# Storing the last column group in two large DMAs, and loading the last weight tile whole, in a windowed matrix product

## The chip, the cores and the metric

The kernel runs on one core of a Trainium2 chip. The metric is the time of one execution on the device, in microseconds (us). The profile of an execution gives a "span", from the first to the last instruction, which is 1.6 to 1.7 us shorter than that time. Engines are called TensorE (matrix products; PE in the profile), VectorE (DVE), ScalarE (ACT), GpSimd (POOL) and SyncE (SP); a "q" behind a name means the engine's instruction stream, where DMAs are issued and semaphores are waited for. A core has 16 DMA engines.

## The reference

```python
x: (4, 4096, 4096) float32;  w: (4096, 4096) float32;  offsets: 4 integers
for b in range(4):
    o = int(offsets[b])
    result[b] = x[b, o:o+64] @ w          # 64 rows of each batch, times the whole of w
```

There are 4 x 64 = 256 rows to multiply. All of `w` (67 MB) has to be read once, so this is work for the DMA engines.

## The kernel before

Two batches share a tile of 128 rows, so there are two row groups `g`. `w` is read as float32 and cast to float16 by the DMA itself, in tiles of 128 rows (`k`) by 2048 columns. There are two column groups `ng` of 2048 columns; each accumulates over 32 `k` tiles in all eight PSUM banks. Loads go through GpSimd's queue. The ends of the two column groups are handled differently: the first is copied to `stage` and stored from GpSimd's queue, behind the last load; the last `k` tile of the second is loaded as four column slices, and each slice is multiplied, copied and stored on its own.

```python
    wlast = []
    for ng in range(n_ng):                       # 2 column groups
        for ki in range(n_k):                    # 32 k tiles
            if (ng, ki) in wh:
                continue
            if ng == n_ng - 1 and ki == n_k - 1:
                for j in range(n_sub):           # the last tile: four slices of 512 columns
                    cs = ng * NG + j * NT
                    t = wl_pool.tile([P, NT], fp16, name=f"wl{j}")
                    nc.gpsimd.dma_start(out=t[:], in_=w[ki * P : (ki + 1) * P, cs : cs + NT])
                    wlast.append(t)
            else:
                wh[(ng, ki)] = load(ng, ki)      # [128, 2048], on GpSimd's queue
    # ... transposes of x; the products of all tiles but the last; the first group's copies to stage ...
    for g in range(G):
        nc.gpsimd.dma_start(out=out[2 * g : 2 * g + 2, :, 0:NG], in_=stage[g][:])
    ki = n_k - 1
    q = [nc.scalar, nc.sync]
    for j in range(n_sub):
        cs = (n_ng - 1) * NG + j * NT
        for g in range(G):
            mm(g, j, ki, wlast[j][:], False, True)
            s = sth_pool.tile([P, NT], fp32, name="sth", tag="sth")
            if g == 0:
                nc.scalar.copy(out=s[:], in_=ps[4 * g + j][:])
            else:
                nc.vector.tensor_copy(out=s[:], in_=ps[4 * g + j][:])
            q[g].dma_start(out=out[2 * g : 2 * g + 2, :, cs : cs + NT], in_=s[:])
```

## Time and profile before

| | |
|---|---|
| time, median of 3 runs | 184.98 us (184.97 to 185.01) |
| span of the profiled execution, which took 184.73 us | 183.1 us |
| TensorE busy | 69% of the span |
| DMA queue of GpSimd | 97% of the DMA engines' span |
| a weight tile of 512 KB lands every | 2.44 us |
| TensorE's work for it | 1.89 us |

The page of the kernel before: the busy tenths of TensorE and of the DMA engines in 40 equal slices of the span, what the DMA engines moved in each, and the chain of waits that ended last, by engine and by line.

```profile
PE   0004799988877777887779878777777877777600
DMA  6999999999999999999999999999999999999994
GB/s 179 348 221 215 207 213 215 215 214 211 213 211 214 215 213 214 214 216 214 211 214 212 213 213 214 213 215 214 215 213 212 213 214 212 213 213 205 387 403 172
...
DMA 90%; issue 2%; ACT 1%; PE 1%; ACTq 1%; POOLq 0%
DMA wh<-in_w_dram 90%; ACT sth L150 1%; PE bank L117 1%; ACTq L153 1%; POOLq L60 0%; POOLq L168 0%
```

The DMA engines are full from the second slice to the last but one; TensorE is not. 90% of the chain is waiting for weight tiles to land. (The GB/s count float16 bytes of a load, half of what is read; that is why the figure doubles when the stores come.)

The timeline of TensorE at the end of the kernel before (start, duration, what ran, what ended the idle time before):

```profile
166.48 1.89 PE L117 MATMUL bank<-wh,xT 128*128 128x512 f16 x8 [0.52 <-DMA wh<-in_w_dram]
168.93 1.89 PE L117 MATMUL bank<-wh,xT 128*128 128x512 f16 x8 [0.57 <-DMA wh<-in_w_dram]
170.65 1.89 PE L117 MATMUL bank<-wl,xT 128*128 128x512 f16 x8
```

Each tile is multiplied at once when it lands, then TensorE idles for half a microsecond. Each of the four slices (`wl`) had landed before TensorE came to it, the last at 171.50 us.

The timeline of the DMA issues for the last group in the kernel before (start, duration of the issue):

```profile
171.69 0.34 ACTq L153 DMA_DIRECT2D out_dram<-sth  x1
172.69 0.35 ACTq L153 DMA_DIRECT2D out_dram<-sth  x1
173.69 0.37 ACTq L153 DMA_DIRECT2D out_dram<-sth  x1
174.71 0.34 ACTq L153 DMA_DIRECT2D out_dram<-sth  x1
172.01 2.12 SPq L153 DMA_DIRECT2D out_dram<-sth  x4
```

The DMA queues of the kernel before from 170 to 175 us, then from 175 to 180 us (packets, MB, share of 16 engines' time). q0 is GpSimd's, q10 ScalarE's and q1 SyncE's:

```profile
q0 software_dynamic: 358, 2.06, 104.0%
q10 hardware_dynamic: 8, 0.02, 0.8%
```

```profile
q10 hardware_dynamic: 519, 0.96, 49.7%
q1 hardware_dynamic: 506, 0.94, 48.5%
q0 software_dynamic: 24, 0.10, 4.8%
```

Though the small stores were issued from 171.7 us on, nearly none of their packets ran before 175 us: until then q0 had the engines with the first group's 2.1 MB.

The stretches view of the kernel before, two microseconds a row (the last two columns are the share of the DMA engines and GB/s):

```profile
core 0: us, PE busy (x) PEld busy (x) DVE busy (x) ACT busy (x) POOL busy (x), PEclk, DMA share, GB/s
170.00:172.00 2.00, 2.00 (x11) 0.93 (x10) 0.71 (x2) 0.58 (x1) 0.00 (x0) 1.00 1.11 400
172.00:174.00 2.00, 0.54 (x3) 0.05 (x1) 1.77 (x3) 1.17 (x2) 0.00 (x0) 1.00 1.03 434
174.00:176.00 2.00, 0.00 (x0) 0.00 (x0) 0.00 (x0) 0.58 (x1) 0.00 (x0) 0.72 0.96 392
176.00:178.00 2.00, 0.00 (x0) 0.00 (x0) 0.00 (x0) 0.00 (x0) 0.00 (x0) 0.50 1.06 409
178.00:180.00 2.00, 0.00 (x0) 0.00 (x0) 0.00 (x0) 0.00 (x0) 0.00 (x0) 0.50 1.04 400
180.00:182.00 2.00, 0.00 (x0) 0.00 (x0) 0.00 (x0) 0.00 (x0) 0.00 (x0) 0.50 0.25 93
```

The tail is full: about 400 GB/s until 180 us. Last, the waits of SyncE's instruction stream at the end of the kernel before (line waiting, what for; us in total, times, longest). L179 is the end of the program, where SyncE waits for every DMA to have landed:

```profile
SPq L179 <- DMA out_dram<-sth: 4.5, 1, 4.5
SPq L179 <- DMA out_dram<-stage: 2.9, 1, 2.9
SPq L179 <- PEq L179: 0.7, 2, 0.5
```

### The profile page before, as it was taken

What the parts mean: (1) busy time and instruction counts of PE and PEld (TensorE: products, weight loads), DVE (VectorE), ACT (ScalarE), POOL (GpSimd) and SP (SyncE); (2) the same over time, 40 slices, a digit from 0 to 9 for tenths busy, and PEclk for the clock granted to TensorE, in tenths of its full rate; (3) what the DMA queues carried; (4) which work ended last, traced back from release to release, by engine and by line L of the source; (5) the groups of instructions that cost most, each with busy time, mean ns of one, the idle gap of its engine ahead of it and who ended that gap; (6) DMA issues with size and microseconds to landing.
All of it is one profiled execution on the core that took longest, in us unless ns stands there. A gap on an engine that the chain in (4) does not pass through costs nothing.

```text
span 183.1 us, 1380 instructions
## 1 busy us (share of the span) xinstructions
PE 126.3 (69%) x576; PEld 56.4 (31%) x576; DVE 10.5 (6%) x16; ACT 14.1 (8%) x19; POOL 38.3 (21%) x77
## 2 busy tenths in 40 slices
PE   0004799988877777887779878777777877777600
PEld 0004664433333233333324333323232333333200
DVE  0002530000000000000005000000000000000500
ACT  2081430000000000000013000000000000000310
POOL 4612221222222112222221222222122222210000
PEclk9999999999999999999999999999999999999965
DMA  6999999999999999999999999999999999999994
GB/s 179 348 221 215 207 213 215 215 214 211 213 211 214 215 213 214 214 216 214 211 214 212 213 213 214 213 215 214 215 213 212 213 214 212 213 213 205 387 403 172
DMA packets 11271, 40.97 MB, mean 224 GB/s; under 512 B 1282, under 2 KB 1794, under 8 KB 10626
## 3 DMA queue, kind: packets, MB, share of 16 engines
q0 software_dynamic: 9968, 36.70, 97.0%
q10 hardware_dynamic: 720, 3.15, 4.7%
q1 hardware_dynamic: 578, 1.05, 1.5%
q8 instruction: 4, 0.07, 0.1%
q14 instruction: 1, 0.01, 0.0%
HBM read 71.30 MB, written 4.19 MB: 412 GB/s over the span
## 4 chain that ended last, share of the span: by engine, by line
DMA 90%; issue 2%; ACT 1%; PE 1%; ACTq 1%; POOLq 0%
DMA wh<-in_w_dram 90%; ACT sth L150 1%; PE bank L117 1%; ACTq L153 1%; POOLq L60 0%; POOLq L168 0%
## 5 line engine op out<-in xcount | busy, mean ns | idle before, releaser
L117 PE MATMUL bank<-wh,xT 128*128 128x512 f16 x488 | 113.8, 378 | 28.6 <-DMA wh<-in_w_dram 28.6
L117 PEld LDWEIGHTS <-xT 128*128 128x128 f16 x512 | 49.8, 97 | 98.0 <-issue 44.1
L60 POOL DMA_DIRECT2D wh<-in_w_dram x61 | 32.4, 531 | 112.5 <-DMA wh<-in_w_dram 100.2
L103 PE MATMUL bank<-identity,xrow 128*128 128x128 f16 x64 | 7.1, 311 | 17.4 <-DMA xrow<-in_x_dram 17.4
L103 PEld LDWEIGHTS <-xrow 128*128 128x128 f16 x64 | 6.7, 147 | 17.6 <-issue 17.6
L150 ACT COPY sth<-bank 128x512 f32<-128x512 f32 x4 | 2.3, 586 | 74.6 <-PE bank L117 73.8
L137 ACT COPY stage<-bank 128x512 f32<-128x512 f32 x4 | 2.1, 600 | 70.5 <-PE bank L117 70.5
L112 DVE CAST xT<-bank 128x512 f16<-128x512 f32 x8 | 5.5, 691 | 19.3 <-PE bank L103 19.3
L152 DVE COPY sth<-bank 128x512 f32<-128x512 f32 x4 | 2.5, 683 | 72.3 <-PE bank L117 72.3
L139 DVE COPY stage<-bank 128x512 f32<-128x512 f32 x4 | 2.5, 682 | 71.7 <-PE bank L117 71.7
L114 ACT CAST xT<-bank 128x512 f16<-128x512 f32 x8 | 4.7, 586 | 6.9 <-PE bank L103 6.9
L117 PE MATMUL bank<-w0half,xT 128*128 128x512 f16 x16 | 4.3, 390 | 0.2 <-DVE stage L139 0.2
L90 POOL DMA_DIRECT2D wl<-in_w_dram x4 | 2.1, 527 | 7.5 <-DMA wh<-in_w_dram 7.5
L77 POOL DMA_DIRECT2D xrow<-in_x_dram x4 | 2.1, 520 | 2.2 <-issue 2.2
L97 ACT CAST w0half<-w0row 128x2048 f16<-128x2048 f32 x1 | 1.9, 1897 | 7.4 <-DMA w0row<-in_w_dram 7.4
L141 POOL DMA_DIRECT2D out_dram<-stage x2 | 1.1, 534 | 4.2 <-DMA wh<-in_w_dram 4.2
L98 ACT CAST w0half<-w0row 128x2048 f16<-128x2048 f32 x1 | 1.9, 1893 | 0.0
L117 PE MATMUL bank<-wl,xT 128*128 128x512 f16 x8 | 1.9, 379 | 0.0
L97 ACT ACT_TABLE_LOAD x1 | 1.3, 1283 | 1.3 <-PEq L168 1.3
masks.py:199 POOL TENSOR_SCALAR_AFFINE_SELECT identity<-identity 128x128 f16<-128x128 f16 x1 | 0.3, 287 | 0.1
masks.py:197 POOL MEMSET identity<- 128x128 f16 x1 | 0.2, 223 | 0.0
L168 POOL MEMSET const-float32-0.0<- 128x1 f32 x1 | 0.1, 98 | 0.4 <-issue 0.4
(3 smaller groups left out, 0.3 us busy)
## 6 DMA issues: line engine op xcount, KB each, us to landing
wh<-in_w_dram POOLq DMA_DIRECT2D x61, 512.0 KB, 19.1
w0row<-in_w_dram ACTq DMA_DIRECT2D x1, 2048.0 KB, 9.0
xrow<-in_x_dram POOLq DMA_DIRECT2D x4, 512.0 KB, 12.3
out_dram<-stage POOLq DMA_DIRECT2D x2, 1024.0 KB, 12.1
out_dram<-sth ACTq DMA_DIRECT2D x4, 256.0 KB, 6.5
out_dram<-sth SPq DMA_DIRECT2D x4, 256.0 KB, 6.6
wl<-in_w_dram POOLq DMA_DIRECT2D x4, 128.0 KB, 14.9
off_t<-in_offsets_dram SPq DMA_DIRECT2D x1, 0.0 KB
```

The source lines that it names most:

```text
L60: nc.gpsimd.dma_start(out=t[:], in_=w[ki * P : (ki + 1) * P, ng * NG : (ng + 1) * NG])
L77: nc.gpsimd.dma_start(out=x16[g][m * WIN : (m + 1) * WIN, :], in_=x[b][bass.ds(o, WIN), :])
L90: nc.gpsimd.dma_start(out=t[:], in_=w[ki * P : (ki + 1) * P, cs : cs + NT])
L97: nc.scalar.copy(out=w0_16[:, :NG], in_=w0_32[:, :NG])
L103: nc.tensor.matmul(out=ps[t][:, i * P : (i + 1) * P], lhsT=x16[g][:, k * P : (k + 1) * P], rhs=identity[:], start=True, stop=True,)
L112: nc.vector.tensor_copy(out=dst, in_=ps[t][:])
L114: nc.scalar.copy(out=dst, in_=ps[t][:])
L117: nc.tensor.matmul(out=ps[4 * g + j][:], lhsT=xT[g][:, ki * P : (ki + 1) * P], rhs=rhs, start=start, stop=stop,)
L137: nc.scalar.copy(out=dst, in_=ps[4 * g + j][:])
L139: nc.vector.tensor_copy(out=dst, in_=ps[4 * g + j][:])
L150: nc.scalar.copy(out=s[:], in_=ps[4 * g + j][:])
L152: nc.vector.tensor_copy(out=s[:], in_=ps[4 * g + j][:])
```

## The change

The intent is fewer and larger DMAs at the end: the last `k` tile comes as one 512 KB load with 4 KB rows in SBUF, and the last column group is copied to a staging tile and stored as two 1 MB DMAs with 8 KB rows. The price is that its stores are issued later. The first group's stores stay where they are, on GpSimd's queue behind the last load.

```diff
-            if ng == n_ng - 1 and ki == n_k - 1:
-                for j in range(n_sub):
-                    ... four loads of 512 columns ...
-            else:
+            if (ng, ki) not in wh:
                 wh[(ng, ki)] = load(ng, ki)
 ...
-    stage = [st_pool.tile([P, NG], fp32, name=f"stage{g}") for g in range(G)]
+    stage = [[st_pool.tile([P, NG], fp32, name=f"stage{ng}{g}") for g in range(G)] for ng in range(n_ng)]
+    q = [nc.scalar, nc.sync]
     for ng in range(n_ng):
         last = ng == n_ng - 1
-        for ki in range(n_k - 1 if last else n_k):
+        for ki in range(n_k):
             ... products ...
-        if not last:
-            ... eight copies to stage ...
-    for g in range(G):
-        nc.gpsimd.dma_start(out=out[2 * g : 2 * g + 2, :, 0:NG], in_=stage[g][:])
-    ... for each slice and g: product, copy to sth, store of 512 columns on q[g] ...
+        ... eight copies to stage[ng] ...
+        for g in range(G):
+            (q[g] if last else nc.gpsimd).dma_start(
+                out=out[2 * g : 2 * g + 2, :, ng * NG : (ng + 1) * NG],
+                in_=stage[ng][g][:],
+            )
```

More of the change, by code (lines that the diff above doesn't have):

```diff
@@ L38 @@
     wh_pool = ctx.enter_context(tc.tile_pool(name="wh", bufs=24))
-    wl_pool = ctx.enter_context(tc.tile_pool(name="wl", bufs=1))
     st_pool = ctx.enter_context(tc.tile_pool(name="st", bufs=1))
-    sth_pool = ctx.enter_context(tc.tile_pool(name="sth", bufs=8))
     psum_pool = ctx.enter_context(tc.tile_pool(name="ps", bufs=1, space=bass.MemoryType.PSUM))
@@ L80 @@
         )
-    wlast = []
     for ng in range(n_ng):
         for ki in range(n_k):
-            if (ng, ki) in wh:
-                continue
-            if ng == n_ng - 1 and ki == n_k - 1:
-                for j in range(n_sub):
-                    cs = ng * NG + j * NT
-                    t = wl_pool.tile([P, NT], fp16, name=f"wl{j}")
-                    nc.gpsimd.dma_start(
-                        out=t[:], in_=w[ki * P : (ki + 1) * P, cs : cs + NT]
-                    )
-                    wlast.append(t)
-            else:
+            if (ng, ki) not in wh:
                 wh[(ng, ki)] = load(ng, ki)
@@ L123, in mm @@
         )
-    stage = [st_pool.tile([P, NG], fp32, name=f"stage{g}") for g in range(G)]
+    stage = [
+        [st_pool.tile([P, NG], fp32, name=f"stage{ng}{g}") for g in range(G)]
+        for ng in range(n_ng)
+    ]
+    q = [nc.scalar, nc.sync]
     for ng in range(n_ng):
         last = ng == n_ng - 1
-        for ki in range(n_k - 1 if last else n_k):
+        for ki in range(n_k):
             for g in range(G):
@@ L131 @@
                     mm(g, j, ki, wh[(ng, ki)][:, j * NT : (j + 1) * NT], ki == 0, ki == n_k - 1)
-        if not last:
-            for j in range(n_sub):
-                for g in range(G):
-                    dst = stage[g][:, j * NT : (j + 1) * NT]
-                    if g == 0:
-                        nc.scalar.copy(out=dst, in_=ps[4 * g + j][:])
-                    else:
-                        nc.vector.tensor_copy(out=dst, in_=ps[4 * g + j][:])
-    for g in range(G):
-        nc.gpsimd.dma_start(out=out[2 * g : 2 * g + 2, :, 0:NG], in_=stage[g][:])
-    ki = n_k - 1
-    q = [nc.scalar, nc.sync]
-    for j in range(n_sub):
-        cs = (n_ng - 1) * NG + j * NT
-        for g in range(G):
-            mm(g, j, ki, wlast[j][:], False, True)
-            s = sth_pool.tile([P, NT], fp32, name="sth", tag="sth")
-            if g == 0:
-                nc.scalar.copy(out=s[:], in_=ps[4 * g + j][:])
-            else:
-                nc.vector.tensor_copy(out=s[:], in_=ps[4 * g + j][:])
-            q[g].dma_start(out=out[2 * g : 2 * g + 2, :, cs : cs + NT], in_=s[:])
+        for j in range(n_sub):
+            for g in range(G):
+                dst = stage[ng][g][:, j * NT : (j + 1) * NT]
+                if g == 0:
+                    nc.scalar.copy(out=dst, in_=ps[4 * g + j][:])
+                else:
+                    nc.vector.tensor_copy(out=dst, in_=ps[4 * g + j][:])
+        for g in range(G):
+            (q[g] if last else nc.gpsimd).dma_start(
+                out=out[2 * g : 2 * g + 2, :, ng * NG : (ng + 1) * NG],
+                in_=stage[ng][g][:],
+            )
 _INS = ['x', 'w', 'offsets']
```

## The prediction

> **What bounds the kernel now.** DMA. The chain of waits puts 90% of the span on weight loads landing, and the page's slices show the DMA engines 90% or more busy almost throughout. In the timeline a 512 KB weight tile lands every 2.44 us and TensorE needs 1.89 us of it. The tail is DMA too: the loads leave the queue at about 170.1 us, then follow 4.19 MB of stores, half from the GpSimd queue (first column group), half from the ScalarE and SyncE queues (last group). In windows of half a microsecond the DMA share stays near 1 from 170 to 180 us; the last packets end near 181.5 us, the span at 183.1 us. 4.19 MB in 10.5 us is 400 GB/s: the tail has almost no hole to fill.
>
> **What changes.**
> - Four 128 KB slices become one 512 KB tile. The slices land over about 2.6 us after the tile before them, a whole tile takes 2.44 us: 0.1 to 0.2 us gained.
> - TensorE could start its last products at 170.65 us. The whole tile lands at about 168.93 + 2.44 = 171.4 us, and its products take 1.89 us. With the copies as in the first group (ScalarE 2.05 us for four, VectorE 2.48 us, starting 0.86 us later), ScalarE issues its 1 MB store at about 173.9 us, SyncE at 175.1 us. Before, the small stores were issued from 171.7 to 174.7 us.
> - Is that lateness paid? In the view of the DMA queues the small stores' first packets ran only at 174.75 us (ScalarE) and 175.25 us (SyncE), some 3.1 us after their issue, when the first-group stores were nearly drained (about 175.2 us). Issuing early bought nothing: they stood behind the 2.1 MB. At the kernel's start, with idle engines, ScalarE's load issued at 0.87 us had packets about 1 us later. With 1 us, the new ScalarE store starts at about 175 us, just as the queue drains, and SyncE's at 176.2 us while ScalarE's runs (2.5 us of data). Hole: 0 to 0.4 us on most engines; those that drain last (packets up to 177 us) see none.
> - Row size: at 171 to 174 us 8 KB rows moved 0.43 MB per us; at 176 to 180 us 2 KB rows moved 0.40. For 2.1 MB that is 4.9 against 5.2 us: 0.3 us gained. The Trainium skill, "DMA: Bandwidth & Descriptors", section "Rules for kernel authors", recommends at least 1 MiB per DMA for bandwidth; this trace shows 8 KB rows only 7% faster. Its section "Issuing engines are not separate DMA queues" says that all queues share the same 16 engines; the trace agrees (shares add to about 100%).
>
> **On the critical path:** gains of 0.3 to 0.5 us, a hole of 0 to 0.4 us, so nearly nothing: estimate 184.9 us, range 184.2 to 186.2; chances 0.02 faster, 0.95 same, 0.03 slower.
>
> **Signs.** Right: last matmuls start at about 171.4 us; stores issue at about 173.9 and 175.1 us; DMA share stays near 1 between 174.5 and 180 us; last packets end within 0.5 us of 181.3 us; the last group's copies take 2.05 and 2.48 us.
>
> **What would make it wrong.** If the 3.1 us from issue to first packet is a fixed cost of such stores and not queueing, the DMA engines idle for nearly 2 us after 175.2 us and the time is about 186. If the big stores spread badly over the engines, the end is ragged. If small loads cost more than I see, it could gain 1 us. A gain over 2% (3.7 us) would need more than any hole that exists; a loss over 2% would need the stores serialised.

## The result, and the profile after

| | before | after |
|---|---|---|
| time, median | 185.00 us (184.97 to 185.09, 4 runs) | 184.12 us (184.09 to 184.15, 4 runs) |
| span of the profiled execution | 183.1 us | 182.5 us |
| DMA packets of the whole execution | 11271 | 9975 |

The ratio is 0.9952 (95% interval 0.9935 to 0.9969). All ratios here are the mean time of one kernel's fast runs over that of the other's of the same rounds, so not quite the ratio of the medians. The gain of 0.88 us is small, well under the 2% (3.7 us) from which the prediction would call a kernel faster, but far outside the spread of the runs. The prediction had expected 0.1 us; the measured time lies 0.08 us below the low end of its range.

The chain of waits, the timeline of TensorE and the issues of the last stores in the changed kernel:

```profile
DMA 90%; issue 3%; DVE 1%; PE 1%; DVEq 0%; POOLq 0%; POOL 0%
```

```profile
169.34 1.89 PE L104 MATMUL bank<-wh,xT 128*128 128x512 f16 x8 [0.58 <-DMA wh<-in_w_dram]
171.82 1.89 PE L104 MATMUL bank<-wh,xT 128*128 128x512 f16 x8 [0.60 <-DMA wh<-in_w_dram]
```

```profile
174.32 0.35 ACTq L131 DMA_DIRECT2D out_dram<-stage  x1
175.61 0.38 SPq L131 DMA_DIRECT2D out_dram<-stage  x1
```

The chain is 90% DMA, as before. The last products start at 171.82 us, the two stores are issued at 174.32 and 175.61 us, each about half a microsecond later than predicted. Most of that is the load phase: the tile before the last was taken up at 169.34 us in this execution, at 168.93 us in the one profiled before. So the spans of the two profiles understate what the tail gained: from that tile to the end of the span there are 183.08 - 168.93 = 14.15 us before and 182.48 - 169.34 = 13.14 us after, 1.0 us less.

The DMA queues of the changed kernel from 170 to 175 and from 175 to 180 us, and its stretches of two microseconds, with the columns as before:

```profile
q0 software_dynamic: 291, 2.02, 99.2%
```

```profile
q10 hardware_dynamic: 144, 1.05, 50.7%
q1 hardware_dynamic: 116, 0.95, 45.2%
q0 software_dynamic: 20, 0.11, 5.1%
```

```profile
170.00:172.00 2.00, 1.40 (x7) 0.57 (x6) 0.00 (x0) 0.00 (x0) 0.00 (x0) 1.00 1.03 399
172.00:174.00 2.00, 1.71 (x8) 0.58 (x6) 0.90 (x2) 1.76 (x4) 0.00 (x0) 1.00 1.00 422
174.00:176.00 2.00, 0.00 (x0) 0.00 (x0) 1.58 (x3) 0.29 (x1) 0.00 (x0) 1.00 0.93 389
176.00:178.00 2.00, 0.00 (x0) 0.00 (x0) 0.00 (x0) 0.00 (x0) 0.00 (x0) 0.73 0.98 406
178.00:180.00 2.00, 0.00 (x0) 0.00 (x0) 0.00 (x0) 0.00 (x0) 0.00 (x0) 0.50 1.06 446
180.00:182.00 2.00, 0.00 (x0) 0.00 (x0) 0.00 (x0) 0.00 (x0) 0.00 (x0) 0.50 0.12 49
```

The tail stays full with late stores too: 0.93 of the engines' time at the handover from 174 to 176 us, against 0.96 before. ScalarE's store, issued at 174.32 us, had its first packet at 175.17 us, 0.85 us later. So the 3.1 us that the small stores had waited were queueing. The Trainium skill, "DMA: Bandwidth & Descriptors", section "Queues, rings and completion order" says of arbitration that a DMA engine takes turns between the queues that have work for it, and drains a whole packet of one, typically 9 to 17 descriptors, before it turns to another. The trace of the kernel before agrees with this only in part. ScalarE's and SyncE's small stores did take turns, 8 rows and a semaphore packet at a time (ScalarE's first store finished on its first engine at 175.39 us, and SyncE's first packet came at 175.40 us). But each DMA engine's part of a first-group store is also only 8 rows, at 0.31 us, and a semaphore packet; the first of these two stores finished on the engines between 172.3 and 173.7 us, when ScalarE's small store, issued at 171.69 us, should have been ready (an estimate with the 0.85 us above: about 172.5 us), and still none of its packets ran before 174.75 us, when the second one began to finish. Why they did not come in between the two is not shown here. In the last stretches the 8 KB rows move 406 and 446 GB/s where the 2 KB rows moved 409 and 400.

The waits of SyncE at the end of the changed kernel:

```profile
SPq L160 <- DMA out_dram<-stage: 5.2, 3, 2.4
SPq L160 <- PEq L160: 0.7, 2, 0.5
```

Here is the part of the gain that the prediction did not have in view. Before, SyncE's last wait for a small store counted as one wait of 4.5 us; after, there are three waits for the stores. The record of SyncE's closing waits, as the traces hold it (us from the start of the span), shows what that means:

```
                              before           after
last store landed             181.78           181.57
waits recorded from then on   7                1
first of the closing drains   182.23           181.65
end of the span               183.08           182.48
from last landing to end        1.30             0.91
```

SyncE goes through the DMA semaphores one instruction at a time, about 0.06 us each, in an order fixed by the program. The DMAs from ScalarE and SyncE take eight semaphores in turn. Before, there were ten such DMAs (two loads at the start and eight stores), so the last two stores used the first two of the eight again. SyncE therefore stood at an early wait until everything had landed, and then had to walk through six further waits, all long satisfied (6 x 0.06 = 0.36 us). After, there are only four such DMAs, and the last to land is also the last to be waited for.

### The profile page after: what moved, and what is told of

Its sections match the earlier page's. It is cut to its first block, busy times and chain, and to the rows that moved or that the text cites. A ratio compares the mean times of both kernels' runs of the same rounds, so it can differ in the third digit from the quotient of the medians.

```text
span 182.5 us, 1369 instructions
## 1 busy us (share of the span) xinstructions
PE 125.0 (69%) x576; PEld 54.7 (30%) x576; DVE 10.2 (6%) x16; ACT 13.5 (7%) x19; POOL 36.8 (20%) x74
## 2 busy tenths in 40 slices
DMA packets 9975, 40.97 MB, mean 225 GB/s; under 512 B 1138, under 2 KB 1138, under 8 KB 9074
## 3 DMA queue, kind: packets, MB, share of 16 engines
q10 hardware_dynamic: 288, 3.15, 4.6%
## 4 chain that ended last, share of the span: by engine, by line
DMA 90%; issue 3%; DVE 1%; PE 1%; DVEq 0%; POOLq 0%; POOL 0%
DMA wh<-in_w_dram 85%; DMA xrow<-in_x_dram 5%; DVE stage L129 1%; PE bank L104 1%; DVEq L160 0%; POOLq L68 0%; POOL identity masks.py:197 0%; POOLq L58 0%; POOLq L75 0%; POOL wh L58 0%; POOLq masks.py:199 0%; POOLq L149 0%
## 5 line engine op out<-in xcount | busy, mean ns | idle before, releaser
L104 PE MATMUL bank<-wh,xT 128*128 128x512 f16 x496 | 116.0, 378 | 31.0 <-DMA wh<-in_w_dram 31.0
L58 POOL DMA_DIRECT2D wh<-in_w_dram x62 | 32.9, 532 | 114.8 <-DMA wh<-in_w_dram 102.5
L90 PE MATMUL bank<-identity,xrow 128*128 128x128 f16 x64 | 5.5, 266 | 17.4 <-DMA xrow<-in_x_dram 17.4
L127 ACT COPY stage<-bank 128x512 f32<-128x512 f32 x8 | 4.1, 600 | 146.5 <-PE bank L104 146.5
L129 DVE COPY stage<-bank 128x512 f32<-128x512 f32 x8 | 5.0, 682 | 146.7 <-PE bank L104 146.7
L90 PEld LDWEIGHTS <-xrow 128*128 128x128 f16 x64 | 5.1, 123 | 17.6 <-issue 17.6
```

The source lines that it names most:

```text
L58: nc.gpsimd.dma_start(out=t[:], in_=w[ki * P : (ki + 1) * P, ng * NG : (ng + 1) * NG])
L90: nc.tensor.matmul(out=ps[t][:, i * P : (i + 1) * P], lhsT=x16[g][:, k * P : (k + 1) * P], rhs=identity[:], start=True, stop=True,)
L104: nc.tensor.matmul(out=ps[4 * g + j][:], lhsT=xT[g][:, ki * P : (ki + 1) * P], rhs=rhs, start=start, stop=stop,)
L127: nc.scalar.copy(out=dst, in_=ps[4 * g + j][:])
L129: nc.vector.tensor_copy(out=dst, in_=ps[4 * g + j][:])
```

## The experiments

The theory: (1) the order of the closing waits is worth 0.3 to 0.4 us; (2) the larger stores save about 0.4 us of packets; (3) the whole load saves 0.1 us; (4) issuing the stores later costs nothing, because the first group's stores fill the DMA engines meanwhile. The rival to (1) is that all of the gain comes from packets; to (3), that the slices cost the full 0.55 us that their packet times suggest; to (4), that the time of issue never mattered.

### The order of the closing waits: four runs

Tiny loads of the offsets, 32 bytes each, at the start of SyncE's queue shift the turn of the eight semaphores and change nothing else.

```diff
     nc.scalar.dma_start(out=w0_32[:], in_=w[0:P, :])
+    for i in range(6):                       # 6 or 8 on the kernel before, 4 or 6 on the changed one
+        dummy = const_pool.tile([1, B], mybir.dt.int64, name=f"dummy{i}")
+        nc.sync.dma_start(out=dummy[:], in_=offsets[None, :])
```

> The kernel before, with six more tiny loads of the offsets (32 bytes each) on the SyncE queue at its start, so that its ten DMAs from ScalarE and SyncE become sixteen and the last two stores no longer take the semaphores that SyncE waits for early in its closing row of waits, but the last ones. Theory A (closing waits: in the trace before, the last store landed at 181.78 us, SyncE then still had seven wait instructions of 0.06 us to go through, the span ended 1.30 us after the landing; in the changed kernel it was 0.91 us): the end comes about 0.9 us after the last landing, and the time is 0.3 to 0.4 us below the kernel before (184.6 us). Theory B (the whole gain comes from the transfers: fewer and larger packets): no change, 185.0 us.

> Control of the run above: eight tiny loads, so that the last two stores take the same two semaphores as in the kernel before. Theory A and theory B both: within 0.1 us of the kernel before (185.0 us). If it is also 0.3 us or more below the kernel before, the tiny loads act through something else (a shift of the load phase) and the run above says nothing of the closing waits.

> Control: the changed kernel with four tiny loads, so that its two big stores take the last two of the eight semaphores. Theory A: the last store is still waited for last, so as the changed kernel, 184.1 us. Theory B: 184.1 us.

> The changed kernel with six tiny loads: its two big stores now take the first two of the eight semaphores again, as the last stores of the kernel before did. Theory A: 0.3 to 0.4 us slower than the changed kernel, 184.4 to 184.5 us, with about 1.3 us between the last landing and the end. Theory B: as the changed kernel, 184.1 us.

| kernel | last stores are waited for | time, median (range) | ratio to before (95%) | last landing to end |
|---|---|---|---|---|
| before | early | 185.00 (184.83 to 185.20) | 1 | 1.30 us |
| before, 6 tiny loads | last | 184.69 (184.50 to 184.72) | 0.9980 (0.9966 to 0.9994) | 0.93 us |
| before, 8 tiny loads | early | 184.97 (184.81 to 185.04) | 0.9996 (0.9982 to 1.0010) | 1.30 us |
| changed, 4 tiny loads | last | 184.06 (184.01 to 184.25) | 0.9952 (0.9938 to 0.9965) | 0.93 us |
| changed, 6 tiny loads | early | 184.48 (184.38 to 184.59) | 0.9972 (0.9958 to 0.9986) | 1.30 us |

SyncE's waits for the small stores, first in the kernel before with six tiny loads, then with eight:

```profile
SPq L182 <- DMA out_dram<-sth: 4.4, 8, 1.1
```

```profile
SPq L182 <- DMA out_dram<-sth: 4.5, 1, 4.5
```

With eight, SyncE waits once, 4.5 us, for a store that lands last, and finds all others done. With six it waits eight times, for one store after another as they land, and nothing is left to walk through. The order is worth 0.3 us on the kernel before and 0.4 us on the changed one, on and off at will, and the tiny loads alone cost nothing that the runs show (184.97 against 185.00 us, 184.06 against 184.12 us). This part of the change's gain has nothing to do with the size of its transfers.

### The two halves of the change: three runs

The first run keeps the four slices of the last tile but stores in two 1 MB DMAs:

```diff
             for g in range(G):                     # in the loop of products of the changed kernel
+            if last and ki == n_k - 1:
+                ... mm(g, j, ki, wlast[j][:], False, True) for each slice j and g ...
```

The second and third load the tile whole but keep the eight small stores (the third with six tiny loads as above):

```diff
-            if ng == n_ng - 1 and ki == n_k - 1:
-                ... four slices ...
             wh[(ng, ki)] = load(ng, ki)
 ...
-            mm(g, j, ki, wlast[j][:], False, True)
+            mm(g, j, ki, wh[(n_ng - 1, ki)][:, j * NT : (j + 1) * NT], False, True)
```

> Half of the change: the last k tile still in four slices of 1 KB rows, but the last group stored as two 1 MB DMAs. The sum in parts says: the loads' slicing costs 0.13 us on the slowest DMA engine (2.61 us from the landing of the tile before to that of the last slice, against 2.48 for a whole tile). Expected 184.1 + 0.13 = 184.25 us. Rival: the packets themselves took 0.098 us per 1 KB row against 0.324 us per 4 KB row, which is 0.55 us more per DMA engine; if that is what counts, 184.65 us.

> The other half: the last k tile whole, but the last group still stored as eight 256 KB DMAs of 2 KB rows, the last two of them on semaphores that the closing waits reach early. If the slicing of the load costs 0.13 us: 184.87 us; if it costs 0.55 us: 184.45 us.

> As the run above with six tiny loads of the offsets, which move the last stores to the semaphores waited for last (found to be worth 0.3 us on the kernel before). What is left against the changed kernel (184.1 us) is then the size of the stores alone. Theory (8 KB rows save 0.43 us of packets and semaphore writes): 184.55 us. Rival (the stores' size is worth nothing, the early issue of the small ones repays it): 184.1 to 184.2 us.

| last load | last stores | waited for | time, median (range) |
|---|---|---|---|
| sliced | 8 small | early (the kernel before) | 185.01 (184.87 to 185.23) |
| whole | 8 small | early | 184.76 (184.69 to 184.93) |
| sliced | 8 small | last (from the runs above) | 184.69 (184.50 to 184.72) |
| whole | 8 small | last | 184.61 (184.41 to 184.75) |
| sliced | 2 large | last | 184.15 (184.07 to 184.34) |
| whole | 2 large | last (the changed kernel) | 184.12 (184.09 to 184.15) |

The size of the stores is worth 184.69 - 184.15 = 0.54 us with the sliced load, and 184.61 - 184.12 = 0.49 us with the whole one. The load is worth 0.03, 0.08 and 0.25 us in its three comparisons: near 0.1 us, and in none of them clear of the spread of the runs. So the 0.55 us that the packets' durations suggest (32 packets of 0.098 us per engine in place of 8 of 0.324 us) is not what the slices cost: their packets overlapped more, as the DMA share of 1.2 in the two microseconds from 168 us shows against 1.06 in the steady state. The landings agree: the last slice landed 2.61 us after the tile before it, the whole tile 2.48 us.

For the stores, the packets do explain most: 64 packets of 0.084 us per engine (2 KB) are 5.38 us, 16 of 0.313 us (8 KB) are 5.01 us, and eight semaphore packets of 0.009 us become two. That makes 0.42 us of the 0.5. Such a sum ignores overlap, and for the slices it misled; here the landings support it. From the landing of the tile before the last to the last landing of all, the four profiled executions took 12.89 us with small and 12.48 us with large stores (sliced load), 12.76 and 12.27 us (whole load): 0.41 and 0.49 us less. Of what remains, up to 0.08 us is again the closing: with small stores waited for last, 0.93 (sliced) and 0.99 us (whole) passed from the last landing to the end, against 0.91 us with large ones. The rest is within the spread of the runs.

### Stores of middle size

```diff
+                if last and c == 1:            # after two of a row group's four copies
+                    cs = ng * NG + s * (NG // 2)
+                    q[g].dma_start(out=out[2 * g : 2 * g + 2, :, cs : cs + NG // 2], in_=half[g][s][:])
```

> The changed kernel with four stores of 512 KB and 4 KB rows, each issued as soon as its two copies are done, about 0.9 us earlier for the first ones. If the cost is per row and per DMA: between the two, about 0.15 us slower than the changed kernel, 184.2 to 184.3 us. If issuing earlier fills a hole: 183.9 us.

The time was 184.21 us (184.18 to 184.30): 0.1 us slower than the changed kernel. Issuing half a store earlier brought nothing; 4 KB rows cost a little, as in the first of the two cases expected.

### Without the filler: two runs

Does a late store really cost nothing, or is its cost only hidden? Both kernels were run with the first group's stores issued from SyncE as soon as they were copied, in the middle of the kernel, so that nothing lies in the queue behind the last load.

```diff
-            (q[g] if last else nc.gpsimd).dma_start(     # the changed kernel
+            (q[g] if last else nc.sync).dma_start(
```
```diff
-        nc.gpsimd.dma_start(out=out[2 * g : 2 * g + 2, :, 0:NG], in_=stage[g][:])   # the kernel before
+        nc.sync.dma_start(out=out[2 * g : 2 * g + 2, :, 0:NG], in_=stage[g][:])
```

> The changed kernel with the first group's two 1 MB stores issued by SyncE as soon as they are copied (near 99 us) instead of from GpSimd's queue behind the last load, so that nothing stands between the last load and the last group's stores. Theory (the later issue of the big stores is hidden only behind that filler): the loads end 5 us later, at about 176.5 us; ScalarE issues its store at about 179.3 us, its packets start 0.85 us later; the DMA engines idle for about 3 us between; 188 us. Rival (the issue time of the last stores does not matter): 184.1 us.

> The kernel before with the same move: first-group stores from SyncE at about 99 us, so no filler behind the last load. Theory (slicing the last tile and the last stores pays when there is no filler): small stores issued from about 176.7 us, packets from about 177.5 us, about 186.3 us, so 1.5 to 2 us faster than the run above, the reverse of the order with the filler. Rival: slicing costs here as it does with the filler, so 0.9 us slower than the run above.

The changed kernel took 188.19 us (188.15 to 188.42), the kernel before 186.84 us (186.79 to 186.94). The stretches from 178 to 182 us, with large stores and then with small ones:

```profile
178.00:180.00 2.00, 0.84 (x4) 0.20 (x2) 1.77 (x3) 1.42 (x3) 0.00 (x0) 1.00 0.00 0
180.00:182.00 2.00, 0.00 (x0) 0.00 (x0) 0.72 (x2) 0.00 (x0) 0.00 (x0) 1.00 0.95 389
```

```profile
178.00:180.00 2.00, 0.00 (x1) 0.00 (x0) 1.23 (x3) 1.14 (x3) 0.00 (x0) 1.00 1.02 380
180.00:182.00 2.00, 0.00 (x0) 0.00 (x0) 0.00 (x0) 0.15 (x1) 0.00 (x0) 0.59 1.02 376
```

The changed kernel came out as expected (188 us). The kernel before was slower than expected (186.3 us), and its lead smaller than the 1.5 to 2 us expected. With large stores the DMA engines were idle from 176.7 us (last load packet) to 180.3 us (first store packet), with small ones from 176.6 to 178.0 us. So without the filler the order of the two kernels turns round: slicing the last load and the last stores is then worth 1.35 us, although the small stores pay more for the closing waits (1.23 against 0.92 us from the last landing to the end). The changed kernel is the faster one only because 2.1 MB of other stores stand behind the last load.

### A faster kernel: larger loads

The changed kernel with 28 pairs of weight tiles, each loaded by one DMA of 1 MB, with single tiles at the start and the end:

```diff
+            t = wp_pool.tile([P, 2, NG], fp16, name="wp", tag="wp")
+            nc.gpsimd.dma_start(
+                out=t[:],
+                in_=w[ki * P : (ki + 2) * P, ng * NG : (ng + 1) * NG].rearrange("(t p) n -> p t n", p=P),
+            )
+            for s in range(2):
+                wh[(ng, ki + s)] = t[:, s, :]
```

> The changed kernel with 28 pairs of weight tiles loaded by one 1 MB DMA each (the same 4 KB rows in SBUF), single tiles kept at the start and the end: 28 DMAs fewer. In the trace each load leaves one 4-byte semaphore packet on each DMA engine, 0.021 us in the mean, and the loads are bound by the DMA engines. If that time counts: 28 x 0.021 = 0.6 us less, 183.5 us. If those packets overlap the others: 184.1 us.

It took 183.47 us (183.40 to 183.52), ratio 0.9916 (0.9903 to 0.9930): 0.65 us better than the changed kernel and 1.5 us better than the kernel before. The packets' rows are the same size, so what it saved is per DMA: 0.65 / 28 = 0.023 us, which is about the time of the 4-byte packet that ends a load on each DMA engine (0.022 us for the loads alone; the 0.021 expected is the mean with the shorter ones of the stores). That this packet is what was saved is the reading that fits; no run changes it alone.

> As the run with pairs (183.47 us), but with 14 loads of four weight tiles (2 MB) each in place of 28 pairs: 14 DMAs fewer again. If the cost per DMA is the 0.021 us of its semaphore packet on each DMA engine: 14 x 0.021 = 0.3 us less, 183.2 us. If coarser loads make TensorE late or leave the queue short near the start: no gain or a loss, 183.5 us or more.

With four tiles to a load it took 186.67 us (186.45 to 188.34, with two of six runs above 188). The timeline of TensorE and of ScalarE's store issue in that kernel:

```profile
166.04 7.07 PE L121 MATMUL bank<-wp,xT 128*128 128x512 f16 x32 [2.77 <-DMA wp<-in_w_dram]
172.94 3.62 PE L121 MATMUL bank<-wh,xT 128*128 128x512 f16 x16
177.17 0.35 ACTq L148 DMA_DIRECT2D out_dram<-stage  x1
```

The last group of four tiles landed at 166.0 us and then needed 7.07 us, and the two single tiles behind them had to wait for that; the store was issued at 177.17 us in place of 174.32 us, its first packet came at 178.02 us, and the filler had run out (its last packet ended at 175.48 us). The DMA engines were busy for 64% of the time from 170 to 180 us. The loads themselves did gain: the last one landed at 170.85 us, against 171.14 us with pairs, which is the 0.3 us expected of 14 DMAs fewer (one execution each).

The granted clock of the whole execution was 0.935, against 0.987 with pairs. But the stretches of this kernel show it near 1 before and during the tail, and the DMA engines full (the third number from the end is the clock, then the DMA share):

```profile
140.00:160.00 20.00, 16.32 (x74) 7.18 (x73) 0.00 (x0) 0.00 (x0) 0.00 (x0) 0.99 1.06 215
160.00:170.00 10.00, 7.23 (x35) 3.20 (x33) 0.00 (x0) 0.00 (x0) 0.00 (x0) 1.00 1.06 229
```

So in the profiled execution the lower clock is not what made the stores late: TensorE even idled for 2.77 us before the last four tiles, and it is the size of that last burst that counts. Of the 3.15 us between the two spans, the last landing accounts for 2.63 us (183.56 against 180.93 us). The other 0.5 us came after it (1.42 against 0.90 us to the end); why, and why two of the six runs took over 188 us, is not shown.

## Why the prediction was wrong

- **What bounds the kernel:** right. The DMA engines, to the end; the tail had no hole to fill.
- **"Issuing early bought nothing":** right. The 3.1 us between issue and first packet were queueing; the large store had packets 0.85 us after its issue (1 us predicted), and the run without the filler shows where the lateness would have been paid.
- **"Hole: 0 to 0.4 us on most engines":** the sum failed here too. The prediction itself said that the engines that drain last see no hole, and those end the kernel: the last landings of the changed kernel follow one another by 2.46, 2.46, 2.48 and 2.39 us. The 0 to 0.4 us should not have been subtracted.
- **"Four 128 KB slices become one 512 KB tile: 0.1 to 0.2 us gained":** right in size; 0.03 to 0.25 us in three comparisons, 0.13 us by landings.
- **"Row size: 0.3 us gained":** under-sized. The stores were worth 0.5 us, of which the packets explain 0.42 and the landings 0.41 to 0.49. The rates, read to two digits from stretches of a few microseconds, were too coarse for this; the packets' own durations give more.
- **The closing waits:** missing from the sum altogether, and worth 0.3 to 0.4 us of the 0.88. The prediction took "last packets end near 181.5 us, the span at 183.1 us" as given and did not ask what fills the time between, nor noticed that the number of DMAs decides which of them is waited for last. This is the step that put the time outside the range: with the old order (six tiny loads) the changed kernel took 184.48 us, which lies inside it. The other 0.4 us up to the estimate of 184.9 us are the hole that was not there and the stores.
- **"If small loads cost more than I see, it could gain 1 us":** near the measured size, but for a reason that did not hold; the whole load is worth only about 0.1 us.
- **Signs:** the copies took 2.05 and 2.48 us, the DMA share stayed near 1 and the last packets ended at 181.2 us, as predicted. The products and stores came 0.4 to 0.5 us later than predicted, of which 0.4 us was the load phase of that execution.

The parts add up: 0.3 to 0.4 us (closing waits), 0.5 us (stores), 0.1 us (load) against 0.88 us measured.

## What to carry to other kernels

When a saturated tail is changed, follow it on the engine that drains last, and then on to the last instruction: after the last landing there is a row of closing waits whose order here depended on how many DMAs ScalarE and SyncE issue, and it was worth 0.3 to 0.4 us, against 0.5 us for the larger stores. Slicing the last load and stores paid where the DMA engines would otherwise have been idle (1.35 us here without the filler), and the small stores cost 0.5 us where other transfers already filled the time. In a kernel that is bound by its loads, halving the number of DMAs at equal row size paid 0.023 us for each DMA saved, until, at four tiles to a load, the coarser grain left TensorE with work behind the last load.

## What the Trainium skill lacked or had wrong

- "DMA: Bandwidth & Descriptors", section "Anatomy of one DMA — SWDGE (gpsimd) path", calls the semaphore write of a DMA essentially free; it speaks of the fixed cost of one DMA. Where loads follow one another without a gap it adds up: the 4-byte packet at the end of each of GpSimd's loads took 0.022 us on each DMA engine, and 28 DMAs fewer saved 0.65 us, 0.023 us each.
- The same page, section "Rules for kernel authors", asks for at least 1 MiB per DMA. In this kernel going from 0.5 to 1 MB per load (as it lands in SBUF; twice that is read) paid 0.65 us, but 2 MB cost 3.2 us against 1 MB; in the profiled executions 2.63 us of that came with the later last landing, since the work behind the last load grew. The rule names no such limit.
- The same page, section "Latency and other measured facts", gives about 600 ns to the first byte for DMAs issued from ScalarE or SyncE. Here the first packet came 0.85 us after the start of the issue instruction, with the DMA engines idle too (177.15 to 177.99 us in the run with small stores and no filler). The issue instruction itself takes 0.34 us of this; the page does not say from where it counts.
- None of the pages tells of the order in which the end of a program waits for its DMAs: 1.30 us against 0.91 to 0.93 us from the last landing to the end of the span.
